# First convolution weights taken in during the attention projection, and a reordered last result

## The chip, the cores and the metric

The kernel runs on one core of a Trainium2 chip. What counts is the time of one execution on the device, in microseconds (us), and less is better. PE is TensorE, the matrix engine; DVE is VectorE, ACT is ScalarE, POOL is GpSimd; SP is the engine that here only issues loads and stores.

## What is computed

Two layers act on 1024 tokens of width 1024, in fp32. The first is windowed attention with a gate, whose output is multiplied by a 2048 x 1024 matrix and added to x. The second is a convolution branch; the part around the change is the end of the first layer and the beginning of the second:

```python
x = x + gate * ((o * silu(z)) @ attn_w_out)        # layer 0: attention
h = rmsnorm(x, norm_g) * (1 + scale) + shift       # layer 1
a, gl, z = split(h @ conv_w_in + conv_b_in, 3)     # 1024 -> 3 x 2048
u = a * sigmoid(gl)
u = conv_depthwise(u, 31 taps) + dw_b
u = silu(layernorm(u)) * silu(z)
x = x + gate * (u @ conv_w_out)
out = rmsnorm(x, final_g)
```

## The kernel before, in words

**Matrix products in three parts.** An fp32 operand is split into a high part (rounded to the matrix engine's fp32r format, a copy on ACT) and a low part (what the rounding left, a subtraction on DVE or POOL). Each product is three matmuls: high x high, high x low, low x high. A 128-wide block of weights is thus loaded ("wraw" for the convolution's input matrix, "wo" for the attention's output matrix), then split into "whi" and "wlo" ("woh" and "wol"). One matmul has 512 columns.

**The attention's output projection (`proj_attn`).** It computes the two halves of the token rows by a scheme of seven products; these are 28 steps: steps i = 0 to 7 are round r = 0, steps 8 to 27 are rounds r = 1 to 5 of four steps (kk = 0 to 3). Each step multiplies one "oz" block (attention output: loaded as "ozf", for some rounds added or subtracted on DVE, split into "ozh" by ACT and "ozl" by DVE) by one "wo" block, into four banks, one for each group of 128 token rows, with six matmuls a bank. `ahead(nl, ns)` loads up to step nl and splits up to step ns. Within `split` the DVE subtraction that makes ozl is not issued at once but put into the list `put_by`; `flush()` issues what is in it. `bgA(r, kk)` is called once for each step and issues background work.

**A finished round.** `first_sum` adds a bank to what earlier rounds left ("part"), `evac0` multiplies by the gate, adds the residual ("xr"), squares and sums on ACT ("junk"; the row sums land in "ssx") and stores the row. `norm0` makes 1/sqrt of the mean square (small operations ms, sq, rr, rq, r on DVE and ACT) and scales the row's two halves into "xn", one half on DVE and one on ACT.

**The last result.** The last product's steps 25 to 27 are held back and run bank by bank (b = 0 to 3), so that a bank's rows can be finished while PE works on the next. After b = 0 and after b = 1 a transposed tile of the first 512 tokens still has to be made.

**Transposed tiles (`turn_in`).** For each of eight k-tiles and each half of the tokens, PE transposes four 128 x 128 pieces of xn into a bank "pso". ACT makes "h2h" (modulated, rounded) and from that "hf", DVE makes "h2l" from the bank and hf. A third pair of transposes has to wait until the first of the two banks is read out. `later` is the list of these to be called.

**The convolution's input projection (`b_mm`).** 48 weight blocks, each for two halves of the tokens, 24 matmuls a block and half. The first five (FIRST) run their first halves, then their second halves; `TURNS` says between which k-steps of blocks 2, 3 and 4 the transposes of the second 512 tokens stand. A block goes to "psg" banks. A gl block is read out by a sigmoid on ACT ("sig"); the a block after it by DVE into "ubuf", whose neighbours POOL then adds ("ubuf" from "ubuf"). The depthwise convolution follows in parts: DVE adds some taps in PSUM ("pss" from "ubuf" with wsum or dww), ACT multiplies the others ("prod"), POOL adds these up ("odd").

**What sets the order.** The order within each engine is fixed when the kernel is built. In the projection (`pin("PVAG")`) PE, DVE, ACT and POOL keep the order of the code; in the first two blocks of the convolution POOL is free to be reordered, and from block 2 on only PE keeps the order. SP's loads may be reordered throughout. Splits of convolution weights have high priority and stand behind the scaling of rows on ACT that came last in the code (`anchor_n`). Tiles come from 45 pages of 1024 words and 6 halves of 528, in the order in which they come free; a load has to wait until its page's last reader is done.

## Time and profile before

| | |
|---|---|
| median of 3 runs | 1689.21 us (1688.74 to 1691.45) |
| the profiled execution | 1689.08 us |
| its span in the trace | 1687.3 us, so 1.8 us lie outside |
| mean granted PE clock | 0.992 |
| busy in the span | PE 1650.8, DVE 1138.4, POOL 931.5, ACT 899.7 us |
| the attention's output projection from step 8 on | about 834 to 953 us |
| convolution blocks 0 and 1, first half | 953.4 to 964.4 us |

Times in the trace run from the start of the span. A row of a timeline gives start, duration, engine, operation, the tile written and the tiles read, and in brackets how long the engine was idle before and which engine's work ended that. A matmul of 512 columns has a row of 0.39 us, but the next one starts about 0.23 us later, since they are pipelined; so PE's pace is read from the distance between starts.

### The profile page before, as it was taken

What the parts mean: (1) busy time and instruction counts of PE and PEld (TensorE: products, weight loads), DVE (VectorE), ACT (ScalarE), POOL (GpSimd) and SP (SyncE); (2) the same over time, 40 slices, a digit from 0 to 9 for tenths busy, and PEclk for the clock granted to TensorE, in tenths of its full rate; (3) what the DMA queues carried; (4) which work ended last, traced back from release to release, by engine and by line L of the source; (5) the groups of instructions that cost most, each with busy time, mean ns of one, the idle gap of its engine ahead of it and who ended that gap; (6) DMA issues with size and microseconds to landing.
All of it is one profiled execution on the core that took longest, in us unless ns stands there. A gap on an engine that the chain in (4) does not pass through costs nothing.

```text
span 1687.3 us, 23985 instructions
## 1 busy us (share of the span) xinstructions
PE 1650.8 (98%) x8244; PEld 1379.1 (82%) x8244; DVE 1138.4 (67%) x2089; ACT 899.7 (53%) x1573; POOL 931.5 (55%) x877
## 2 busy tenths in 40 slices
PE   9999999999999999999999879999999999999998
PEld 6888888888888888888788658888888888888886
DVE  5755544555354554556477789999999998868722
ACT  6644543555355544556228486555656554566831
POOL 0338774686458674772110089999889887130400
PEclk9999999999999999999999989999999999999999
DMA  9435553564356653577778412020211202377971
GB/s 383 167 92 165 157 171 94 166 194 143 96 166 194 197 156 117 170 226 254 273 268 327 152 50 89 13 75 13 76 50 51 82 34 80 130 269 249 320 285 50
DMA packets 151321, 263.53 MB, mean 156 GB/s; under 512 B 46122, under 2 KB 62818, under 8 KB 151200
## 3 DMA queue, kind: packets, MB, share of 16 engines
q1 hardware_dynamic: 142816, 247.84, 43.9%
q10 hardware_dynamic: 8384, 14.16, 2.9%
q8 instruction: 65, 1.06, 0.3%
q14 instruction: 56, 0.46, 0.1%
HBM read 197.19 MB, written 54.27 MB: 149 GB/s over the span
## 4 chain that ended last, share of the span: by engine, by line
PE 85%; DMA 4%; POOL 3%; DVE 3%; ACT 2%; issue 2%; ACTq 0%; SPq 0%; POOLq 0%; DVEq 0%
PE psg L94 45%; PE pso L94 21%; PE pss L94 19%; DMA rope_half<-rope_half 2%; POOL rope_half L94 1%; DVE x_page L94 1%; POOL lhi_half L94 1%; DMA wraw_page<-in_k_win_dram 1%; POOL wlo_page L94 1%; DMA wo_page<-wslow 0%; POOL ql_page L94 0%; DMA araw_page<-in_k_ada_dram 0%; POOL p_page L94 0%; ACT whi_page L94 0%; DVE pss L94 0%
## 5 line engine op out<-in xcount | busy, mean ns | idle before, releaser
L94 POOL TENSOR_TENSOR odd_half<-odd_half,prod_half 128x513 f32<-128x513 f32 (+2 forms) x252 | 317.0, 1264 | 17.7 <-ACT prod_half L94 3.7
L94 PE MATMUL psg<-hh_page,whi_page 128*128 128x512 f32 x600 | 236.8, 395 | 0.0
L94 PE MATMUL psg<-hl_page,whi_page 128*128 128x512 f32 x600 | 234.8, 391 | 0.0
L94 PE MATMUL psg<-hh_page,wlo_page 128*128 128x512 f32 x600 | 234.3, 391 | 0.0
L94 ACT ACTIVATE prod_half<-ubuf,dww 128x513 f32<-128x513 f32 (+2 forms) x252 | 164.9, 674 | 124.8 <-POOL odd_half L94 118.6
L94 POOL TENSOR_TENSOR wlo_page<-wraw_page,whi_page 128x512 fp32r<-128x512 f32 (+1 forms) x104 | 170.8, 1659 | 107.5 <-ACT whi_page L94 103.9
L94 PE MATMUL psg<-h2h_page,whi_page 128*128 128x512 f32 x464 | 183.0, 394 | 11.1 <-ACT whi_page L94 11.1
L94 PE MATMUL psg<-h2h_page,wlo_page 128*128 128x512 f32 x464 | 181.5, 391 | 4.5 <-POOL wlo_page L94 4.5
L94 PE MATMUL psg<-h2l_page,whi_page 128*128 128x512 f32 x464 | 181.3, 391 | 0.0
L94 DVE SCALAR_TENSOR_TENSOR pss<-ubuf,wsum,pss 128x512 f32<-128x512 f32 (+3 forms) x270 | 174.2, 674 | 1.4
L94 DVE SCALAR_TENSOR_TENSOR pss<-ubuf,dww,pss 128x512 f32<-128x512 f32 (+3 forms) x270 | 173.9, 674 | 1.4
L94 ACT ACTIVATE pt<-pss 128x640 fp32r<-128x640 f32 (+1 forms) x128 | 86.5, 676 | 140.3 <-PE pss L94 127.8
L94 POOL TENSOR_SCALAR p_page<-p_page,sc 128x576 f32<-128x576 f32 (+2 forms) x128 | 93.2, 729 | 98.2 <-DVE sc L94 94.0
L94 DVE CUSTOM_DVE_ANT_0 p_page<-pss,mask_page,nsink 128x576 f32<-128x576 f32 (+1 forms) x112 | 90.2, 805 | 75.9 <-PE pss L94 57.3
L94 ACT ACTIVATE p_page<-p_page,sc 128x577 f32<-128x577 f32 (+2 forms) x128 | 96.9, 757 | 68.0 <-DVE sc L94 66.0
L94 PEld LDWEIGHTS psg<-hh_page,wlo_page 128*128 128x128 f32 x600 | 112.7, 188 | 24.4 <-POOL wlo_page L94 0.3
L94 DVE TENSOR_TENSOR pt<-pss,pt 128x640 fp32r<-128x640 f32 (+1 forms) x128 | 100.7, 787 | 44.2 <-ACT pt L94 43.9
L94 PEld LDWEIGHTS psg<-hh_page,whi_page 128*128 128x128 f32 x600 | 112.8, 188 | 19.7 <-ACT hh_page L94 0.3
L94 PEld LDWEIGHTS psg<-hl_page,whi_page 128*128 128x128 f32 x600 | 113.1, 188 | 19.1 <-DVE hl_page L94 0.2
L94 PE MATMUL pso<-h2h_page,whi_page 128*128 128x512 f32 x304 | 118.3, 389 | 0.0
L94 PE MATMUL pso<-h2l_page,whi_page 128*128 128x512 f32 x304 | 118.3, 389 | 0.0
L94 PE MATMUL pso<-h2h_page,wlo_page 128*128 128x512 f32 x304 | 118.3, 389 | 0.0
(294 smaller groups left out, 3980.6 us busy)
## 6 DMA issues: line engine op xcount, KB each, us to landing
wraw_page<-in_k_wconv_dram SPq DMA_DIRECT2D x48, 512.0 KB, 3.3
wraw_page<-in_k_win_dram SPq DMA_DIRECT2D x40, 512.0 KB, 4.2
wo_page<-in_conv_w_out_dram SPq DMA_DIRECT2D x32, 512.0 KB, 5.7
wol_page<-wolC SPq DMA_DIRECT2D x32, 512.0 KB, 5.9
ozf_page<-ozd SPq DMA_DIRECT2D x28, 512.0 KB, 7.1
...
araw_page<-in_k_ada_dram SPq DMA_DIRECT2D x16, 512.0 KB, 10.0
...
```

Of the source, the lines that this page charges most:

```text
L94: r = f(*a, **k)
```

## The change

Four things are changed.

1. The first four blocks of the convolution's weights (0 to 3) are loaded and split at set steps of rounds 1 to 5, by a table of steps. Blocks 4 and 5 are loaded in round 5. Before, blocks 0 and 1 were loaded at the end of round 4 and split in round 5, and blocks 2 to 5 were loaded and split in the loop of the first five blocks, behind the last result. The low parts of blocks 0 to 3 are all made by POOL, in two pieces; before, DVE made those of blocks 0 and 1, and POOL those of 2 to 5. In the blocks' loop there is no split after block 0 any more.
2. `flush()` is called after `ahead` in steps 4 to 7, and after the call of `ahead(10, 9)` ahead of step 8. So step 8's ozl is issued ahead of the first sums of round 0.
3. In the last result, a transposed tile's low part (h2l) comes behind the bank's sums, and the rows are normed by pairs (banks 0 and 1, then 2 and 3) with `rstd_of`, no longer one by one; `rstd_one` is gone.
4. "hf" is one of the 6 halves, no longer a page; the pages of "sig" and "zsb" are taken behind the projection.

```diff
+AHEAD_B = {(1, 3): ("load",), (2, 1): ("split", "load"), (2, 3): ("split", "load"), (3, 1): ("split",), (3, 2): ("load",),
+           (5, 2): ("split", "load", "load")}
...
-    def rstd_one(ssum, n, part):
...
@@ WStream.split
-                    split_lo(self.lo_eng(i), l, r, h)
+                    for a in range(0, KT, KT // 2 if i < 4 else KT):
+                        sl = slice(a, a + (KT // 2 if i < 4 else KT))
+                        split_lo(self.lo_eng(i), *(t[:, sl] for t in (l, r, h)))
@@ proj_attn, round 0
                 ahead(*LOAD_TO[i])
+                flush()
...
         ahead(10, 9)
+        flush()
@@ proj_attn, last result
                             run(block(n, b, acc[b]))
-                        if b < 2:
-                            later.popleft()()
+                        low = later.popleft()(True) if b < 2 else None
                         first_sum(1, 0, b, acc[b], part("m", b), True)
                         evac0(1, 0, b, xr, acc[b])
-                        norm0(1, 0, b)
+                        if low:
+                            low()
+                        if b % 2:
+                            norm0(1, 0, (b - 1, b + 1))
@@ norm0
-        if at is None:
-            r = rstd_of(ss[1], D, 4, ss[0])
-            rows = [(b, r[:, b:b + 1]) for b in range(4)]
-        else:
-            rows = [(at, rstd_one(ss[1][:, at:at + 1], D, ss[0][:, at:at + 1]))]
+        b0, b1 = span
+        r = rstd_of(ss[1][:, b0:b1], D, b1 - b0, ss[0][:, b0:b1])
+        rows = [(b, r[:, b - b0:b - b0 + 1]) for b in range(b0, b1)]
@@ turn_in
-        f = pg.alloc(F32, [1024], "hf")
+        f = hp.alloc(F32, None, "hf")
...
-            stt(H2l[(h, kt)], tv, mod1[:, 8 + kt:9 + kt], fv, ALU.mult, ALU.subtract)
-        pg.free(f)
+
+        def low():
+            with tc.high_priority():
+                stt(H2l[(h, kt)], tv, mod1[:, 8 + kt:9 + kt], fv, ALU.mult, ALU.subtract)
+            hp.free(f)
+
...
+        if hold:
+            return low
+        low()
@@ the convolution's weights
-    wsB = WStream(hp=True, lo_eng=lambda i: V if i < 2 or i % 3 == 0 and i > 3 else G, srcs=...)
+    wsB = WStream(hp=True, lo_eng=lambda i: V if i % 3 == 0 and i > 3 else G, srcs=...)
@@ bgA
-        if (r, kk) == (4, 3):
-            wsB.load()
-            wsB.load()
-        if r == 5:
-            if kk != 1:
-                wsB.split()
+        for what in AHEAD_B.get((r, kk), ()):
+            getattr(wsB, what)()
@@ the first five blocks
         b_mm(i, 0)
         wsB.load()
-        wsB.split()
+        if i:
+            wsB.split()
         wsB.load()
```

PE's own instructions stand in the same order before and after. Three places show how the others move.

**Place 1: DVE at the end of round 0.** The x rows are the first sums of the four banks of step 7; ozl_page_8590 before and ozl_page_8516 after are the low part for step 8 (made from ozf_page_8387 and ozf_page_8385). Before:

```order
L94 TENSOR_TENSOR ozf_page_8387<-ozf_page_8385,ozf_page_8387 128x1024
L94 TENSOR_TENSOR x_page_8542<-psg_7972,part_page_8186 128x512
L94 TENSOR_TENSOR x_page_8542<-psg_7973,part_page_8186 128x512
L94 TENSOR_TENSOR x_page_8557<-pss_8377,part_page_8439 128x512
L94 TENSOR_TENSOR x_page_8557<-pss_8378,part_page_8439 128x512
L94 TENSOR_TENSOR ozf_page_8470<-ozf_page_8468,ozf_page_8470 128x1024
L94 TENSOR_TENSOR ozf_page_8532<-ozf_page_8530,ozf_page_8532 128x1024
L94 TENSOR_TENSOR ozl_page_8590<-ozf_page_8387,ozh_page_8511 128x1024
```

And after:

```order
L96 TENSOR_TENSOR ozf_page_8385<-ozf_page_8383,ozf_page_8385 128x1024
L96 TENSOR_TENSOR ozl_page_8516<-ozf_page_8385,ozh_page_8509 128x1024
L96 TENSOR_TENSOR x_page_8542<-psg_7972,part_page_8186 128x512
L96 TENSOR_TENSOR x_page_8542<-psg_7973,part_page_8186 128x512
L96 TENSOR_TENSOR x_page_8557<-pss_8375,part_page_8437 128x512
L96 TENSOR_TENSOR x_page_8557<-pss_8376,part_page_8437 128x512
L96 TENSOR_TENSOR ozf_page_8468<-ozf_page_8466,ozf_page_8468 128x1024
L96 TENSOR_TENSOR ozl_page_8576<-ozf_page_8468,ozh_page_8569 128x1024
```

Step 8's ozl moved from behind the four sums and two additions to ahead of them; step 9's stands behind its own addition.

**Place 2: DVE in the last result.** psg_7972 is bank 0 and psg_7973 bank 1; h2l are the low parts of the transposed tiles, x and xn the rows. Before, from the first sum of bank 0 to that of bank 1:

```order
L94 SCALAR_TENSOR_TENSOR h2l_page_9440<-pso_9441,mod_611,hf_page_9446 128x512
L94 TENSOR_TENSOR psg_7972<-psg_7972,part_page_8186 128x512
L94 TENSOR_TENSOR psg_7972<-psg_7972,gate_page_8353 128x512
L94 TENSOR_TENSOR x_page_9450<-psg_7972,xr_page_9411 128x512
L94 TENSOR_SCALAR ms_599_9457<-ssx_595_9341,ssx_594_9340 128x1
L94 RECIPROCAL rr_601_9459<-sq_600_9458 128x1
L94 TENSOR_SCALAR rq_602_9460<-rr_601_9459 128x1
L94 TENSOR_SCALAR rq_602_9460<-rq_602_9460,ms_599_9457 128x1
L94 TENSOR_SCALAR r_603_9466<-rq_602_9460,rr_601_9459 128x1
L94 TENSOR_SCALAR xn_page_9468<-x_page_9450,r_603_9466 128x512
L94 SCALAR_TENSOR_TENSOR h2l_page_9440<-pso_9490,mod_611,hf_page_9495 128x512
L94 TENSOR_TENSOR psg_7973<-psg_7973,part_page_8186 128x512
```

After, the same stretch and on to the scaling of both rows:

```order
L96 TENSOR_TENSOR psg_7972<-psg_7972,part_page_8186 128x512
L96 TENSOR_TENSOR psg_7972<-psg_7972,gate_page_8353 128x512
L96 TENSOR_TENSOR x_page_9467<-psg_7972,xr_page_9424 128x512
L96 SCALAR_TENSOR_TENSOR h2l_page_9458<-pso_9459,mod_611,hf_half_9464 128x512
L96 TENSOR_TENSOR psg_7973<-psg_7973,part_page_8186 128x512
L96 TENSOR_TENSOR psg_7973<-psg_7973,gate_page_8353 128x512
L96 TENSOR_TENSOR x_page_9467<-psg_7973,xr_page_9424 128x512
L96 SCALAR_TENSOR_TENSOR h2l_page_9458<-pso_9493,mod_611,hf_half_9498 128x512
L96 SCALAR_TENSOR_TENSOR ms_600_9508<-ssx_595_9358,ssx_594_9357 128x2
L96 RECIPROCAL rr_602_9512<-sq_601_9510 128x2
L96 SCALAR_TENSOR_TENSOR rq_603_9514<-rr_602_9512 128x2
L96 TENSOR_TENSOR rq_603_9514<-rq_603_9514,ms_600_9508 128x2
```

The sums of bank 1 moved ahead of the norm of bank 0, one chain of small operations serves two rows, and each h2l stands behind its bank's sums.

**Place 3: ACT and POOL behind the last scaled row.** sig is the first gl block's sigmoid, the whi rows are weight copies (before: blocks 5, 4, 2, then 3; after: blocks 6, 5, 7, then 4 and 8), h2h_page_9705 before and h2h_page_9693 after the first transposed tile of the second 512 tokens. ACT before:

```order
L94 ACTIVATE sig_page_8375<-psg_9595,vt 128x512
L94 ACTIVATE whi_page_9848<-wraw_page_9693 128x1024
L94 ACTIVATE whi_page_9771<-wraw_page_9687 128x1024
L94 ACTIVATE whi_page_9623<-wraw_page_9621 128x1024
L94 ACTIVATE odd_half_9656<-ubuf,vt,dww 128x249
L94 ACTIVATE prod_half_9658<-ubuf,dww 128x249
L94 ACTIVATE prod_half_9661<-ubuf,dww 128x249
L94 ACTIVATE prod_half_9664<-ubuf,dww 128x249
L94 ACTIVATE prod_half_9667<-ubuf,dww 128x249
L94 ACTIVATE prod_half_9670<-ubuf,dww 128x249
L94 ACTIVATE whi_page_9689<-wraw_page_9627 128x1024
L94 ACTIVATE prod_half_9719<-ubuf,dww 128x249
L94 ACTIVATE prod_half_9722<-ubuf,dww 128x249
L94 ACTIVATE h2h_page_9705<-pso_9707,mod_611 128x512
```

ACT after:

```order
L96 ACTIVATE sig_page_9591<-psg_9593,vt 128x512
L96 ACTIVATE whi_page_9836<-wraw_page_9681 128x1024
L96 ACTIVATE whi_page_9759<-wraw_page_9437 128x1024
L96 ACTIVATE whi_page_9908<-wraw_page_9763 128x1024
L96 ACTIVATE odd_half_9646<-ubuf,vt,dww 128x249
L96 ACTIVATE prod_half_9648<-ubuf,dww 128x249
L96 ACTIVATE prod_half_9651<-ubuf,dww 128x249
L96 ACTIVATE prod_half_9654<-ubuf,dww 128x249
L96 ACTIVATE prod_half_9657<-ubuf,dww 128x249
L96 ACTIVATE prod_half_9660<-ubuf,dww 128x249
L96 ACTIVATE whi_page_9677<-wraw_page_9435 128x1024
L96 ACTIVATE h2h_page_9693<-pso_9695,mod_611 128x512
L96 ACTIVATE whi_page_10132<-wraw_page_9840 128x1024
L96 ACTIVATE h2h_page_9693<-pso_9723,mod_611 128x512
```

POOL at the same place, before:

```order
L94 TENSOR_TENSOR wol_page_8631<-wo_page_8580,woh_page_8629 128x512 x2
L94 TENSOR_TENSOR ubuf<-ubuf 128x263
L94 TENSOR_TENSOR wlo_page_9849<-wraw_page_9693,whi_page_9848 128x1024
L94 TENSOR_TENSOR wlo_page_9772<-wraw_page_9687,whi_page_9771 128x1024
L94 TENSOR_TENSOR wlo_page_9624<-wraw_page_9621,whi_page_9623 128x1024
L94 TENSOR_TENSOR odd_half_9656<-odd_half_9656,prod_half_9658 128x249
L94 TENSOR_TENSOR wlo_page_9690<-wraw_page_9627,whi_page_9689 128x1024
L94 TENSOR_TENSOR odd_half_9656<-odd_half_9656,prod_half_9661 128x249
```

and after:

```order
L96 TENSOR_TENSOR wlo_page_8908<-wraw_page_8823,whi_page_8907 128x512 x2
L96 TENSOR_TENSOR wlo_page_9026<-wraw_page_8912,whi_page_9025 128x512 x2
L96 TENSOR_TENSOR wlo_page_9431<-wraw_page_9066,whi_page_9430 128x512 x2
L96 TENSOR_TENSOR wlo_page_9760<-wraw_page_9437,whi_page_9759 128x1024
L96 TENSOR_TENSOR wlo_page_9909<-wraw_page_9763,whi_page_9908 128x1024
L96 TENSOR_TENSOR ubuf<-ubuf 128x263
L96 TENSOR_TENSOR odd_half_9646<-odd_half_9646,prod_half_9648 128x249
L96 TENSOR_TENSOR wlo_page_9678<-wraw_page_9435,whi_page_9677 128x1024
L96 TENSOR_TENSOR odd_half_9646<-odd_half_9646,prod_half_9651 128x249
```

The copies for blocks 2 and 3 are gone from here, and those for blocks 6, 5 and 7 stand in their place ahead of the first products. On POOL the low parts of blocks 5 and 7 stand ahead of the first ubuf, which before came first.

23 lines of the change are left out of this document (7 added, 16 removed).

## The prediction

> **What bounds the kernel now.** I read the page's busy row first, then PE's waits, then PE's timeline around each of them, and then the timelines of the engines that were waited for. The page's row of busy time, and the waits of PE from 820 to 1010 us (how long in all, how often, the longest):
>
> ```profile
> PE 1650.8 (98%) x8244; PEld 1379.1 (82%) x8244; DVE 1138.4 (67%) x2089; ACT 899.7 (53%) x1573; POOL 931.5 (55%) x877
> PE psg L94 <- ACT whi_page L94: 11.1, 1, 11.1
> PE psg L94 <- POOL wlo_page L94: 4.5, 1, 4.5
> PE pso L94 <- DVE ozl_page L94: 3.7, 1, 3.7
> PE pso L94 <- DVE h2l_page L94: 0.8, 2, 0.4
> ```
>
> PE bounds the kernel. Its matmuls are the same after the change, so a gain can only come from its waits, and from what follows a wait. The timeline of PE shows both:
>
> ```profile
> 834.60 0.39 PE L94 MATMUL pso<-woh_page,ozh_page 128*128 128x512 f32 x1
> 834.82 0.39 PE L94 MATMUL pso<-wol_page,ozh_page 128*128 128x512 f32 x1
> 838.95 0.79 PE L94 MATMUL pso<-woh_page,ozl_page 128*128 128x512 f32 x1 [3.74 <-DVE ozl_page L94]
> 839.54 0.63 PE L94 MATMUL pso<-woh_page,ozh_page 128*128 128x512 f32 x1
> 839.96 0.63 PE L94 MATMUL pso<-wol_page,ozh_page 128*128 128x512 f32 x1
> ...
> 953.48 0.39 PE L94 MATMUL psg<-h2h_page,whi_page 128*128 128x512 f32 x1
> ...
> 964.13 0.39 PE L94 MATMUL psg<-h2h_page,wlo_page 128*128 128x512 f32 x1
> 975.64 0.79 PE L94 MATMUL psg<-h2h_page,whi_page 128*128 128x512 f32 x1 [11.12 <-ACT whi_page L94]
> 976.23 0.63 PE L94 MATMUL psg<-h2l_page,whi_page 128*128 128x512 f32 x1
> 981.32 0.80 PE L94 MATMUL psg<-h2h_page,wlo_page 128*128 128x512 f32 x1 [4.46 <-POOL wlo_page L94]
> 981.91 0.63 PE L94 MATMUL psg<-h2h_page,whi_page 128*128 128x512 f32 x1
> 982.34 0.63 PE L94 MATMUL psg<-h2l_page,whi_page 128*128 128x512 f32 x1
> ...
> 985.71 0.39 PE L94 MATMUL psg<-h2l_page,whi_page 128*128 128x512 f32 x1
> ```
>
> A matmul normally starts 0.23 us after the last one (834.60 to 834.82). The row at 953.48 is the first matmul of the convolution's block 0, so bank 3 of the last result is finished there. From 834.82 to 838.95 it is 4.1 us, so 3.9 too long; then about eight are 0.2 us too slow (839.54 to 839.96: 0.42), 1.7 us together. I call this stall A: 5.6 us. From 964.13 to 975.64 it is 11.5 us (11.3 too long), from 976.23 to 981.32 5.1 us (4.9 too long), and up to 985.7 matmuls stand 0.43 us apart (981.91 to 982.34): 2.6 us too long in all. With the two h2l waits of 0.8 us this is stall B: 11.3 + 4.9 + 2.6 + 0.8 = 19.6 us. If all went and nothing came in its place, the gain would be 25.2 us.
>
> The third view is the busy time by stretches (us, then PE, PEld, DVE, ACT, POOL, and PE's granted clock):
>
> ```profile
> 964.00:1004.00 40.00, 23.61 (x105) 17.98 (x104) 32.12 (x68) 30.14 (x53) 26.14 (x25) 0.79 0.12 41
> 1004.00:1400.00 396.00, 396.00 (x1748) 327.89 (x1747) 387.85 (x589) 233.62 (x328) 355.01 (x259) 1.00 0.16 56
> ```
>
> Behind stall B, PE does not wait for 396 us, but DVE is busy for 387.85 of them (98%) and POOL for 355. In the convolution there is a second engine that is nearly the bound. This is what limits the gain from B.
>
> **Stall A: `flush()`.** DVE, ACT and POOL around it:
>
> ```profile
> 835.40 2.35 DVE L94 TENSOR_TENSOR ozf_page<-ozf_page,ozf_page 128x1024 f32<-128x1024 f32 x2
> 837.67 4.58 DVE L94 TENSOR_TENSOR ozl_page<-ozf_page,ozh_page 128x1024 fp32r<-128x1024 f32 x3
> ...
> 837.66 1.04 ACT L94 ACTIVATE woh_page<-wo_page 128x1024 fp32r<-128x1024 f32 x1
> ...
> 828.21 2.53 POOL L94 TENSOR_TENSOR wol_page<-wo_page,woh_page 128x512 fp32r<-128x512 f32 x2 [19.11 <-ACT woh_page L94]
> 838.78 12.57 POOL L94 TENSOR_TENSOR wol_page<-wo_page,woh_page 128x512 fp32r<-128x512 f32 x6 [8.04 <-ACT woh_page L94]
> ```
>
> PE waits for step 8's ozl (837.67, behind the sums and two additions), which now stands ahead of the sums. So PE goes through step 8 without a wait: 24 matmuls from 834.6, to 840.0. Step 9 is late next: its addition still stands behind the last sum (835.4), ACT's woh runs from 837.7 to 838.7, and POOL's two halves of wol start at 838.8. Alone such a half takes 1.27 us (828.21), beside a busy DVE 2.1 us (838.78: 12.57 by 6), so they are done at 840.9 and 843.0 at most, while PE wants them at 840.3 and 841.6. The new wait is 0 to 2.1 us; I take 2.0, the value beside a busy DVE, since DVE stays busy there. It is under the 3.7 us behind which matmuls were slow. Gain from A: 5.6 - 2.0 = 3.6 us.
>
> **Stall B: weights split earlier, and the last result reordered.** DVE's first and last operations in the last result, and what follows on ACT and POOL:
>
> ```profile
> 946.82 1.22 DVE L94 TENSOR_TENSOR wlo_page<-wraw_page,whi_page 128x1024 fp32r<-128x1024 f32 x1 [0.78 <-ACT whi_page L94]
> 948.24 0.75 DVE L94 SCALAR_TENSOR_TENSOR h2l_page<-pso,mod,hf_page 128x512 fp32r<-128x512 f32 x1 [0.20 <-ACT hf_page L94]
> 948.90 0.69 DVE L94 TENSOR_TENSOR psg<-psg,part_page 128x512 f32<-128x512 f32 x1
> 960.89 0.69 DVE L94 TENSOR_TENSOR pss<-pss,part_page 128x512 f32<-128x512 f32 x1
> 965.66 0.69 DVE L94 TENSOR_TENSOR pss<-pss,part_page 128x512 f32<-128x512 f32 x1
> 972.78 0.75 DVE L94 SCALAR_TENSOR_TENSOR ubuf<-psg,vt,sig_page 128x512 f32<-128x512 f32 x1 [2.27 <-ACT sig_page L94]
> 974.36 0.54 DVE L94 TENSOR_SCALAR pss<-ubuf,wsum,dwb 128x248 f32<-128x248 f32 x1 [0.31 <-POOL ubuf L94]
> ...
> 970.77 1.28 ACT L94 ACT_TABLE_LOAD   x1
> 972.65 2.94 ACT L94 ACTIVATE whi_page<-wraw_page 128x1024 fp32r<-128x1024 f32 x3
> 975.98 2.06 ACT L94 ACTIVATE prod_half<-ubuf,dww 128x249 f32<-128x249 f32 x5
> ...
> 973.68 0.65 POOL L94 TENSOR_TENSOR ubuf<-ubuf 128x263 f32<-128x263 f32 x1 [122.33 <-DVE ubuf L94]
> 974.28 6.98 POOL L94 TENSOR_TENSOR wlo_page<-wraw_page,whi_page 128x1024 fp32r<-128x1024 f32 x3
> ```
>
> Before, a row costs 4.8 us (sum to sum, 960.89 to 965.66), the last xn is out at 970.77, when ACT loads its table, and block 2's whi comes third behind that on ACT, its wlo third on POOL. After, blocks 2 and 3 are split in the projection or early in the last result; POOL's 122 us of idle time and ACT's gaps there hide this (eight halves of 1.27 to 2.1 us, four copies of about 1 us). Were that cover gone, they would cost 10 to 21 us, on an engine that PE waits for only through wol. DVE's two weight subtractions of 1.2 us go.
>
> I walk the last result with these durations. The first sum stood at 948.9 behind the two subtractions, a wait of 0.8 us for the second one's copy, and an h2l of 0.7 us; without them it starts at 948.9 - 2.4 - 0.8 - 0.7 = 945.0. Three operations a bank take 2.2 us, an h2l 0.7, and a norm, from a bank's third operation to the last xn, 3 us (967.8 to 970.8), with a second row 3.5. That gives 950.1 for bank 1's sums, 953.6 for the first pair, 958.0 for bank 3's sums (PE ended bank 3 at 953.5) and, a norm later, about 961.2 for the last xn, 9.6 us earlier than before. The table load and the sigmoid take 1.9 us (970.77 to 972.65) and end at 963.1, before PE is done with block 1 (964.4). The waits of 11.1 and 4.5 us and the slow matmuls go.
>
> What is late next? ACT has whi of blocks 6, 5 and 7 ahead of the first products: to 966.1. POOL has wlo of blocks 5 and 7 (2.3 us each, 6.98 by 3) ahead of the first ubuf: 965.1 to 969.7, ubuf until 970.3. So DVE's second tap starts at 970.3, where it was 974.36: only 4.1 us earlier. On ACT an odd, the five products, block 4's copy, h2h, block 8's copy, the second h2h, a sigmoid and hf follow. I give those without a row of their own the sigmoid's 0.6 to 0.7 us: 966.1 + 0.5 + 2.1 + 1.0 + 0.7 + 1.0 + 0.7 + 0.7 + 0.7 = 973.5, and the first h2l on DVE is done at 974.2. PE reaches the third transposes, which need that bank, at about 970.7 (24 matmuls and two sets of transposes behind 964.4). This is a new wait of up to 3.5 us (nothing if ACT gets through sooner). The fourth transposes wait for an hf that now waits for POOL's odd sums in the halves: about 1.0 us, an estimate from POOL's order, and the second half of block 0 about 0.7 us, one h2l. Together 5.2 us, with bounds 0 and 8.
>
> A clock loss of 1.7 us followed the 3.74 us gap of stall A, while the waits for h2l of 0.4 us show none. 3.5 us is nearer the former; but my 3.5 us is itself an upper value, so I take half, 0.9 us. The Trainium skill ("TensorE: Matmul & The Clock Gate", Part 1) says that PE falls to half its clock after an idle window of about 3.4 us that runs freely, and needs about as long to come back. The 3.74 us gap agrees with that. By this rule the new wait would drop the clock or not, as the window falls; with a drop the time below would be 1675.4 in place of 1674.6 us.
>
> Gain from B: 19.6 - 5.2 - 0.9 = 13.5 us. With A, PE has 17.1 us at about 1005.
>
> **What the convolution gives back.** DVE begins its taps only 4.1 + 3.6 = 7.7 us earlier, and has 8.15 us of idle time in the 396 us to catch up with. At the end of the convolution stands
>
> ```profile
> 1436.12 1.23 DVE L94 TENSOR_TENSOR wlo_page<-wraw_page,whi_page 128x1024 fp32r<-128x1024 f32 x1
> 1443.47 6.67 DVE L94 TENSOR_TENSOR v_page<-v_page,pso 128x512 f32<-128x512 f32 x11 [6.13 <-PE pso L94]
> ```
>
> DVE waits 6.1 us for PE there. So if DVE catches up by nothing, 7.7 + 6.1 = 13.8 us are kept; if it catches up, all 17.1. I take 14.6, near the lower end, since a DVE at 98% has little to catch up with. 1689.08 - 14.6 = 1674.5 for the profiled execution; the median of the runs is 0.1 above it, so 1674.6 us.
>
> **The rivals.** Bounds for a verdict: 0.2% is 3.4 us, about what a measurement of this kernel can tell from no change.
>
> First: *DVE and POOL bound the convolution from the start.* If the banks run out in the middle, the 6.1 us at the end cannot be used, and the gain is what DVE's start gains: 7.7 us, 1681.4 (6 to 11 us: 1678 to 1683). For it: 98% busy, and POOL's wlo ahead of ubuf. Against: 396 us without one wait of PE, so that there is some room.
>
> Second: *the new waits do not come*, because ACT and POOL get through sooner or the reordered taps let DVE catch up: 19 to 24 us, 1665 to 1670. Against: the products' and weight copies' places in the order of ACT.
>
> Third: *the stall only moves.* If the transposes and their low parts, and not the weights, are what PE needs, block 2's wait of 11 us turns up at the third transposes. It would have to be over 16 us for no change; my walk gives 3.5. The time would be about 1689 us.
>
> Fourth, slower: *block 6's weights come late.* ACT's copy of them stands first behind the sigmoid, ahead of everything that PE waits for, and its load stands in SP's queue behind one that waits until PE has finished bank 3 (953.5), and waits itself for the first xn (953.5). Landing takes
>
> ```profile
> wraw_page<-in_k_wconv_dram SPq DMA_DIRECT2D x48, 512.0 KB, 3.3
> ```
>
> 3.3 us, so it is there at 957, or at 963 if three such loads share the queue; ACT wants it at 963.1. Every us later is one more at the third transposes. From 14.6 us later on (978) it is slower than before; 20 us later would give 1689.1 + 5.4 = 1694.5. Against it: that is six times the row's 3.3 us.
>
> **How the numbers follow.** Forecast (12 to 18 us, 1671 to 1677): 0.50. First rival: 0.25. Second: 0.12. Third, within 0.2%: 0.07. Fourth and the like: 0.06. Range: 1667.5 (the greater part of the second rival) to 1684 (all of the first); outside are the third and fourth rivals and the second's end, under 0.2. Faster by over 0.2%: 0.50 + 0.25 + 0.12 = 0.87; same 0.07; slower 0.06.
>
> **What would show it.** In the profile after: no PE wait for whi or wlo at block 2; at step 9 a wait for wol of about 2 us in place of 3.7 for ozl; the last xn about 10 us earlier; a wait for h2l of 1 to 3.5 us at the third transposes; DVE's idle time ahead of the vsum matmuls shorter than 6.1 us. It is wrong if PE waits in the convolution behind 1005 us for ubuf, or for whi of block 6 or later.

## The result, and the profile after

| | before | after |
|---|---|---|
| median, us | 1690.07 (4 runs, 1688.74 to 1691.45) | 1675.65 (4 runs, 1674.76 to 1676.35) |
| profiled execution, us | 1689.08 | 1676.35 |
| span in the trace, us | 1687.3 | 1674.6 |
| mean granted PE clock | 0.992 | 0.996 |

The ratio is 0.9914, with a 95% interval of 0.9897 to 0.9932. By the medians that is a gain of 14.4 us; the spans of the two profiled executions differ by 12.7 us, and the account below goes by these. Executions of one kernel lie up to 2.7 us apart in this table, so a difference of 1 us between two single traces says little. The prediction was 1674.6 us. It was near, but its terms were wrong in opposite directions, as the trace shows.

The page's row of busy time, and the waits of PE from 815 to 1010 us (how long in all, how often, the longest), in the changed kernel:

```profile
PE 1650.0 (99%) x8244; PEld 1379.0 (82%) x8244; DVE 1130.9 (68%) x2077; ACT 900.9 (54%) x1571; POOL 932.1 (56%) x883
PE pso L96 <- DVE h2l_page L96: 4.8, 2, 2.5
PE pso L96 <- POOL wol_page L96: 1.2, 1, 1.2
PE psg L96 <- DVE ozl_page L96: 1.1, 1, 1.1
PE psg L96 <- ACT woh_page L96: 1.0, 1, 1.0
```

The waits for whi (11.1 us) and wlo (4.5) are gone, and that for ozl at step 8 (3.7). The wol wait of step 9 is there, as foreseen. But three waits stand in the middle of the projection, where the kernel before had none. PE's timeline gives their places:

```profile
842.97 0.50 PE L96 MATMUL pso<-wol_page,ozh_page 128*128 128x512 f32 x1 [1.25 <-POOL wol_page L96]
...
887.00 0.50 PE L96 MATMUL psg<-woh_page,ozh_page 128*128 128x512 f32 x1 [0.97 <-ACT woh_page L96]
894.32 0.50 PE L96 MATMUL psg<-woh_page,ozl_page 128*128 128x512 f32 x1 [1.11 <-DVE ozl_page L96]
...
927.63 0.66 PE L96 MATMUL pso<-ident,xn_page 128*128 128x128 f32 x4 [2.52 <-DVE h2l_page L96]
928.94 0.63 PE L96 MATMUL pss<-woh_page,ozh_page 128*128 128x512 f32 x1
929.37 0.63 PE L96 MATMUL pss<-wo_page,ozh_page 128*128 128x512 f32 x1
...
956.69 0.39 PE L96 MATMUL psg<-h2h_page,whi_page 128*128 128x512 f32 x1
...
976.37 1.07 PE L96 MATMUL pso<-ident,xn_page 128*128 128x128 f32 x4 [2.24 <-DVE h2l_page L96]
977.67 0.63 PE L96 MATMUL psg<-h2l_page,whi_page 128*128 128x512 f32 x1
978.09 0.63 PE L96 MATMUL psg<-h2h_page,wlo_page 128*128 128x512 f32 x1
```

The number to take from this is the start of block 0, 956.69. Before it was 953.48. So PE comes out of the projection 3.2 us later than before, not 3.6 us earlier: the waits of 0.97, 1.11 and 2.52 us and the matmuls at half pace behind the last of them (928.94 to 929.37) have used up what step 8 gave, and more. Of these 3.2 us, 0.6 were there at step 8 already: PE reached it at 835.18, before at 834.60. That is no effect of the change that the runs show, since in the runs below PE reaches step 8 at 834.5 to 836.2, with and without the flushes. From step 8 to block 0 it took 121.5 us, 2.6 more than the 118.9 before. From block 0 on, however, PE gains 15.9 us, since it ends 12.7 us earlier. The one wait left there is the foreseen one, at the third transposes (2.24 us, and slow matmuls again).

Why do these transposes wait? ACT, POOL and DVE of the changed kernel behind the last result, each in order of time:

```profile
962.88 1.28 ACT L96 ACT_TABLE_LOAD   x1
964.17 0.69 ACT L96 ACTIVATE sig_page<-psg,vt 128x512 f32<-128x512 f32 x1
964.75 2.94 ACT L96 ACTIVATE whi_page<-wraw_page 128x1024 fp32r<-128x1024 f32 x3
...
974.82 0.72 ACT L96 ACTIVATE hf_half<-h2h_page,bcol 128x512 f32<-128x512 f32 x1
...
966.83 4.86 POOL L96 TENSOR_TENSOR wlo_page<-wraw_page,whi_page 128x1024 fp32r<-128x1024 f32 x2 [16.17 <-ACT whi_page L96]
...
972.33 0.54 DVE L96 TENSOR_SCALAR pss<-ubuf,wsum,dwb 128x248 f32<-128x248 f32 x1 [3.30 <-POOL ubuf L96]
975.57 0.75 DVE L96 SCALAR_TENSOR_TENSOR h2l_page<-pso,mod,hf_half 128x512 fp32r<-128x512 f32 x1 [0.63 <-ACT hf_half L96]
```

The three weight copies start as soon as the sigmoid is done, so their loads had landed: block 6's weights are not late. POOL's two low parts (4.86 us) stand ahead of the first sum of ubuf's neighbours, and DVE waits 3.30 us for that. The hf for the transposes is done only at 975.5, behind copies and products on ACT, and the h2l behind that. This is the chain that the prediction walked.

The stretches of the changed kernel (PE, PEld, DVE, ACT, POOL, clock), and the end of the convolution, where DVE writes vsum, PE multiplies it and DVE goes on with the product (first the kernel before, L94, then the changed one, L96):

```profile
964.00:1004.00 40.00, 37.76 (x175) 30.93 (x174) 31.50 (x66) 33.63 (x59) 30.55 (x32) 0.96 0.10 32
1004.00:1400.00 396.00, 396.00 (x1748) 327.89 (x1747) 384.20 (x589) 232.81 (x324) 348.17 (x255) 1.00 0.16 56
...
1435.39 0.69 DVE L94 TENSOR_TENSOR vsum_page<-vsum_page,v_page 128x512 f32<-128x512 f32 x1
1442.41 1.02 PE L94 MATMUL pso<-vsum_page,ones 128*128 128x512 f32 x2
...
1428.21 0.69 DVE L96 TENSOR_TENSOR vsum_page<-vsum_page,v_page 128x512 f32<-128x512 f32 x1
1429.71 1.02 PE L96 MATMUL pso<-vsum_page,ones 128*128 128x512 f32 x2
1430.77 3.67 DVE L96 TENSOR_TENSOR v_page<-v_page,pso 128x512 f32<-128x512 f32 x6 [1.86 <-PE pso L96]
```

Of the first 40 us PE was busy for 23.61 before and is for 37.76 now. In the 396 us behind them PE has no wait in either kernel, and nothing of the lead is given back. DVE's idle time behind vsum fell from 6.13 to 1.86 us. More exactly, vsum was ready 6.3 us before PE took it (1436.08 to 1442.41) and is ready 0.8 us before now (1428.90 to 1429.71).

### The profile page after: what moved, and what is told of

It is laid out like the page before. It is cut to its first block, busy times and chain, and to the rows that moved or that the text cites. A ratio compares the mean times of both kernels' runs of the same rounds, so it can differ in the third digit from the quotient of the medians.

```text
span 1674.6 us, 23971 instructions
## 1 busy us (share of the span) xinstructions
PE 1650.0 (99%) x8244; PEld 1379.0 (82%) x8244; DVE 1130.9 (68%) x2077; ACT 900.9 (54%) x1571; POOL 932.1 (56%) x883
## 4 chain that ended last, share of the span: by engine, by line
PE 85%; DMA 4%; DVE 3%; POOL 3%; issue 2%; ACT 2%; ACTq 0%; SPq 0%; POOLq 0%; DVEq 0%
PE psg L96 46%; PE pso L96 21%; PE pss L96 19%; DMA rope_half<-rope_half 2%; DMA wo_page<-wsums 1%; POOL rope_half L96 1%; DVE ozl_page L96 1%; POOL lhi_half L96 1%; DVE ozf_page L96 1%; DVE x_page L96 1%; DMA dww_raw<-in_ada_w_dram 0%; DMA ozf_page<-ozd 0%; ACT ozh_page L96 0%; POOL ql_page L96 0%; DMA xr_page<-in_x_dram 0%
## 5 line engine op out<-in xcount | busy, mean ns | idle before, releaser
L96 POOL TENSOR_TENSOR odd_half<-odd_half,prod_half 128x513 f32<-128x513 f32 (+2 forms) x252 | 312.5, 1248 | 31.6 <-ACT prod_half L96 18.7
L96 POOL TENSOR_TENSOR wlo_page<-wraw_page,whi_page 128x512 fp32r<-128x512 f32 (+1 forms) x110 | 179.1, 1645 | 214.9 <-ACT whi_page L96 165.0
L96 PE MATMUL psg<-hh_page,whi_page 128*128 128x512 f32 x600 | 236.8, 395 | 0.0
L96 PE MATMUL psg<-hl_page,whi_page 128*128 128x512 f32 x600 | 234.8, 391 | 0.0
L96 PE MATMUL psg<-hh_page,wlo_page 128*128 128x512 f32 x600 | 234.3, 391 | 0.0
L96 ACT ACTIVATE prod_half<-ubuf,dww 128x513 f32<-128x513 f32 (+2 forms) x252 | 165.3, 674 | 105.1 <-POOL odd_half L96 101.6
L96 PE MATMUL psg<-h2h_page,whi_page 128*128 128x512 f32 x464 | 182.5, 393 | 0.0
L96 PE MATMUL psg<-h2h_page,wlo_page 128*128 128x512 f32 x464 | 181.1, 390 | 0.0
L96 PE MATMUL psg<-h2l_page,whi_page 128*128 128x512 f32 x464 | 181.1, 390 | 0.0
L96 DVE SCALAR_TENSOR_TENSOR pss<-ubuf,wsum,pss 128x512 f32<-128x512 f32 (+3 forms) x270 | 173.5, 673 | 1.0
L96 DVE SCALAR_TENSOR_TENSOR pss<-ubuf,dww,pss 128x512 f32<-128x512 f32 (+3 forms) x270 | 173.4, 673 | 1.0
L96 ACT ACTIVATE pt<-pss 128x640 fp32r<-128x640 f32 (+1 forms) x128 | 86.5, 676 | 139.1 <-PE pss L96 126.4
L96 POOL TENSOR_SCALAR p_page<-p_page,sc 128x576 f32<-128x576 f32 (+2 forms) x128 | 93.4, 730 | 97.5 <-DVE sc L96 96.4
L96 DVE CUSTOM_DVE_ANT_0 p_page<-pss,mask_page,nsink 128x576 f32<-128x576 f32 (+1 forms) x112 | 90.2, 805 | 75.6 <-PE pss L96 57.1
L96 ACT ACTIVATE p_page<-p_page,sc 128x577 f32<-128x577 f32 (+2 forms) x128 | 96.9, 757 | 68.3 <-DVE sc L96 66.4
L96 PEld LDWEIGHTS psg<-hh_page,wlo_page 128*128 128x128 f32 x600 | 112.7, 188 | 24.5 <-POOL wlo_page L96 0.3
L96 DVE TENSOR_TENSOR pt<-pss,pt 128x640 fp32r<-128x640 f32 (+1 forms) x128 | 100.7, 787 | 43.9 <-ACT pt L96 43.5
L96 PEld LDWEIGHTS psg<-hh_page,whi_page 128*128 128x128 f32 x600 | 112.8, 188 | 19.7 <-ACT hh_page L96 0.3
L96 PEld LDWEIGHTS psg<-hl_page,whi_page 128*128 128x128 f32 x600 | 113.1, 188 | 19.0 <-DVE hl_page L96 0.2
L96 PE MATMUL pso<-h2h_page,whi_page 128*128 128x512 f32 x304 | 118.3, 389 | 0.0
L96 PE MATMUL pso<-h2l_page,whi_page 128*128 128x512 f32 x304 | 118.3, 389 | 0.0
L96 PE MATMUL pso<-h2h_page,wlo_page 128*128 128x512 f32 x304 | 118.3, 389 | 0.0
```

Of the source, the lines that this page charges most:

```text
L96: r = f(*a, **k)
```

## The experiments

Theory A: taking the weights in early is not free in the projection; GpSimd's subtractions beside VectorE, ACT's copies, or the pages held cost PE 6 to 7 us by block 0. Its rival is that the flushes or the new order of the last result make the new waits. Theory B: the lead behind block 0 is limited only by the order on ACT and POOL at the first transposes. Its rival is the prediction's first one, that DVE bounds the convolution, so that a larger lead would be lost there.

All runs, each with the kernel before on the same chip. "Block 0" is the start of its first matmul in the trace, "from step 8" the time from step 8's first matmul to it. The second is the better measure of the projection, since PE's arrival at step 8 differs by up to 1.7 us between these single executions.

| kernel | block 0, us | from step 8, us | span, us | median, us | before there, us | ratio (95% interval) |
|---|---|---|---|---|---|---|
| before | 953.48 | 118.9 | 1687.3 | | 1690.07 | |
| after | 956.69 | 121.5 | 1674.6 | 1675.65 | 1690.07 | 0.9914 (0.9897 to 0.9932) |
| e1 flushes alone | 950.30 | 115.0 | 1684.1 | 1686.27 | 1690.65 | 0.9974 (0.9964 to 0.9984) |
| e2 weights alone | 959.95 | 125.2 | 1687.3 | 1689.00 | 1690.65 | 0.9989 (0.9980 to 0.9998) |
| e3 order alone | 954.75 | 120.2 | 1679.4 | 1681.56 | 1690.65 | 0.9943 (0.9929 to 0.9956) |
| e4 after without flushes | 961.72 | 125.5 | 1679.1 | 1679.80 | 1690.65 | 0.9937 (0.9924 to 0.9951) |
| e5 after without weights | 950.99 | 115.0 | 1675.9 | 1677.36 | 1689.62 | 0.9925 (0.9912 to 0.9939) |
| e6 weights late | 950.58 | 115.0 | 1672.9 | 1674.93 | 1689.62 | 0.9912 (0.9899 to 0.9926) |
| e7 copies behind first turns | 956.59 | 121.3 | 1678.8 | 1679.88 | 1689.62 | 0.9941 (0.9928 to 0.9953) |
| e8 e6 and e7 together | 949.76 | 115.0 | 1672.9 | 1675.49 | 1689.62 | 0.9917 (0.9904 to 0.9931) |
| e9 copies behind all turns | 950.39 | 115.0 | 1667.7 | 1669.61 | 1691.39 | 0.9876 (0.9861 to 0.9890) |
| e10 e9 with hf in pages | 950.03 | 115.1 | 1666.3 | 1668.61 | 1691.39 | 0.9870 (0.9855 to 0.9885) |
| e11 e6 with early loads | 950.90 | 115.0 | 1673.3 | 1674.62 | 1691.39 | 0.9903 (0.9887 to 0.9920) |
| e12 after without low parts | 952.63 | 117.4 | 1670.5 | 1672.38 | 1690.63 | 0.9893 (0.9877 to 0.9910) |

### The change in its parts: e1 to e5

**e1**, the kernel before with the flushes.

```diff
@@ before, proj_attn
                 ahead(*LOAD_TO[i])
+                flush()
...
         ahead(10, 9)
+        flush()
```

> The kernel before with the two calls of flush alone. Theory: the matrix engine's new waits of the projection in the changed kernel (about 1.0 us for woh, 1.1 for ozl, 2.5 for h2l with slow matmuls behind it) come from the weights that are loaded and split there. Then this kernel has the whole gain of stall A, 3.5 us by the traces, and keeps it to the end: about 1686.5 us. Rival: they come because the matrix engine runs 3.5 us ahead of engines that had no slack. Then the same waits stand here, the gain is lost by 930 us, and the time is that of before within 1 us: about 1689.

The waits of PE:

```profile
PE psg L94 <- ACT whi_page L94: 11.1, 1, 11.1
...
PE pso L94 <- POOL wol_page L94: 1.2, 1, 1.2
```

PE starts block 0 3.2 us earlier and keeps just that to the end (spans 1687.3 and 1684.1). From step 8 on it gains 3.9 us. None of the new waits in the projection is there, so the flushes do not make them.

**e2**, the kernel before with the early weights alone (the table of steps, the low parts on POOL in pieces, sig and zsb taken late).

```diff
@@ before, bgA
-        if (r, kk) == (4, 3):
-            wsB.load()
-            wsB.load()
-        if r == 5:
-            if kk != 1:
-                wsB.split()
+        for what in AHEAD_B.get((r, kk), ()):
+            getattr(wsB, what)()
@@ the first five blocks
-        wsB.split()
+        if i:
+            wsB.split()
```

> The kernel before with the weights of blocks 0 to 3 loaded and split in the projection (and the two pages taken later), without flush and with the last result in its old order. Theory: weights alone do not do it, since block 2 needs the bank that the first sigmoid reads, and that stands behind the last scaled row (972.8 us in the trace of before). The matrix engine then waits about 8 us there for the sigmoid in place of 11.1 and 4.5 for weights: 4 to 8 us gained, about 1683. Rival: the weights are what was waited for, and the gain of B comes from them alone: 12 us or more, under 1678.

The ratio's interval reaches 0.9998, so nearly nothing came of it. Block 0 starts 6.5 us later than before, and the wait at block 2 is now one for the sigmoid, which stands behind the last norm:

```profile
977.99 0.79 PE L96 MATMUL psg<-h2h_page,whi_page 128*128 128x512 f32 x1 [7.00 <-ACT sig_page L96]
```

The expectation was too good: it had seen the later sigmoid, but not the price in the projection.

**e3**, the kernel before with the order alone.

```diff
@@ before, last result
-                        if b < 2:
-                            later.popleft()()
+                        low = later.popleft()(True) if b < 2 else None
                         first_sum(1, 0, b, acc[b], part("m", b), True)
                         evac0(1, 0, b, xr, acc[b])
-                        norm0(1, 0, b)
+                        if low:
+                            low()
+                        if b % 2:
+                            norm0(1, 0, (b - 1, b + 1))
@@ turn_in
-        f = pg.alloc(F32, [1024], "hf")
+        f = hp.alloc(F32, None, "hf")
```

> The kernel before with the last result reordered and normed by pairs (and hf in the halves) alone. Theory: the last scaled row comes 9 us earlier, so block 2's high part comes about 9 us earlier, and its low part, third on GpSimd, about 7 us earlier: the two waits shrink from 15.6 to about 7 us and 7 to 10 us are gained, about 1681. Rival: the weights alone set block 2, and the order saves nothing that the matrix engine sees: 1689.

7.9 us of span, as expected: the wait for whi falls from 11.1 to 2.6 us, while that for wlo is still 4.1. Block 0 comes 1.3 us later than before, but not because of the order: behind the same wait of 3.7 us at step 8, 13 matmuls stood 0.42 to 0.43 us apart here and 6 in the kernel before.

**e4**, the changed kernel without the flushes.

```diff
@@ after, proj_attn
                 ahead(*LOAD_TO[i])
-                flush()
...
         ahead(10, 9)
-        flush()
```

> The changed kernel without the two calls of flush. Theory (the projection's new waits come from the weights): the wait of 3.7 us for ozl of step 8 is back with its slow matmuls, 5.6 us, and the 1.3 us for wol goes; later waits stay for the most part: 2 to 4 us slower than the changed kernel, about 1679. Rival (they come from running ahead): what flush wins is lost by 930 us anyway, and the time is that of the changed kernel within 1 us, 1675.7.

4.5 us of span are lost again (1.1 of them before step 8), where 2 to 4 were expected; the ozl wait of 3.7 is back, and ozl 1.1, woh 0.7 and h2l stay. Against e3, which differs from it in the weights only, block 0 comes 5.3 us later from step 8 on.

**e5**, the changed kernel with the weights taken in as before.

```diff
@@ after, bgA
-        for what in AHEAD_B.get((r, kk), ()):
-            getattr(wsB, what)()
+        if (r, kk) == (4, 3):
+            wsB.load()
+            wsB.load()
+        if r == 5:
+            if kk != 1:
+                wsB.split()
```

> The changed kernel without the early weights: flush and the reordered last result alone, the weights of blocks 0 to 5 loaded and split as before. If the parts simply add up, it gains 4.4 + 9.1 us by the runs of each alone: about 1677 us. Theory: the early weights bring little in the end, since what they save at block 2 (2.6 us for the high part and 4.1 for the low part are left in the run with the order alone, with slow matmuls behind) they take in the projection (about 6.5 us): within 2 us of the changed kernel, 1675 to 1678. Rival: the early weights are the core of the gain: 1681 or more.

```profile
PE psg L94 <- POOL wlo_page L94: 4.2, 1, 4.2
PE psg L94 <- ACT whi_page L94: 2.6, 1, 2.6
```

The waits in the projection are gone, those for whi and wlo are back with 6.8 us. The median is 1.7 us above that of the changed kernel. So the early weights are worth only 1.3 us of span (0.5 from step 8 on), and the intervals of the two ratios overlap; flushes and order bring 11.4 of the 12.7 us. Three pairs that differ in the early weights alone (e2 and before, after and e5, e4 and e3) put their price from step 8 to block 0 at 6.3, 6.5 and 5.3 us. The pairs differ in how many slow matmuls followed their waits. e1 and e5, with and without the order, take the same 115.0 us, so the order costs nothing there.

### What in the early weights costs: e6, e11, e12

**e6**, the changed kernel with the first blocks loaded and split late, in rounds 4 and 5.

```diff
-AHEAD_B = {(1, 3): ("load",), (2, 1): ("split", "load"), (2, 3): ("split", "load"), (3, 1): ("split",), (3, 2): ("load",),
-           (5, 2): ("split", "load", "load")}
+AHEAD_B = {(4, 3): ("load", "load"), (5, 0): ("split", "load"), (5, 2): ("split", "split", "load", "load")}
@@ the first five blocks
-        if i:
-            wsB.split()
+        wsB.split()
```

> The changed kernel with the weights taken in later: blocks 0 and 1 loaded at the end of round 4 as before, blocks 0 to 2 split at steps (5, 0) and (5, 2), block 3 in the loop of the first five blocks. Theory: the projection's new waits (woh 1.0, ozl 1.1, h2l 2.5, slow matmuls 1.5 us, about 6 us) go with the weights of rounds 1 to 3, and block 2 does not wait: 1669 to 1672 us. Block 3's low part, now behind others on GpSimd, may take 1 to 3 us of it. Rival: the convolution on VectorE bounds what comes behind, and gives it back: 1675.

```profile
PE pso L95 <- DVE h2l_page L95: 5.9, 2, 5.3
PE pso L95 <- POOL wol_page L95: 1.2, 1, 1.2
```

Block 0 starts at 950.58, 6.1 us earlier than in the changed kernel, and only step 9's wait for wol is left in the projection. But the time is 1674.93, not 1669 to 1672. That is the rival's number, yet not by its mechanism, since PE does not wait behind 1005 us: PE reaches the third transposes sooner, and the wait there grows from 2.24 to 5.34 us. The expectation had taken that wait as fixed. POOL shows why it is not:

```profile
965.51 0.67 POOL L95 TENSOR_TENSOR ubuf<-ubuf 128x263 f32<-128x263 f32 x1
966.12 5.85 POOL L95 TENSOR_TENSOR wlo_page<-wraw_page,whi_page 128x1024 fp32r<-128x1024 f32 x3
971.93 0.71 POOL L95 TENSOR_TENSOR odd_half<-odd_half,prod_half 128x249 f32<-128x249 f32 x1
```

Now three weight blocks (5.85 us) stand between the first ubuf and the first sum of products. On ACT, the hf of the third transposes starts behind that sum.

**e11**, e6 with the loads of blocks 0 and 1 early, but their splits late.

```diff
-AHEAD_B = {(4, 3): ("load", "load"), (5, 0): ("split", "load"), (5, 2): ("split", "split", "load", "load")}
+AHEAD_B = {(1, 3): ("load",), (2, 1): ("load",), (5, 0): ("split", "load"), (5, 2): ("split", "split", "load", "load")}
```

> The kernel with the late weights, with the loads of blocks 0 and 1 alone put back to where the change has them (rounds 1 and 2), their splits still in round 5. Tells apart what makes the matrix engine wait in the projection. If the loads do it (SyncE's queue and the pages they hold): waits for woh, ozl or h2l of 1 us or more stand in rounds 3 to 5 again, 1677 to 1680 us. If the splits do it (ScalarE's copies, GpSimd's low parts beside VectorE): no such wait, and the time of the kernel with the late weights, 1675.

Block 0 starts at 950.90 and the projection has no wait but step 9's: early loads of blocks 0 and 1 cost nothing. That leaves the splits, with the pages that split blocks hold; the early loads of blocks 2 and 3 were not tried alone.

**e12**, the changed kernel in which POOL only writes zeros for the low parts of blocks 0 to 2 (their subtraction is left out).

```diff
@@ after, WStream.split
-                        split_lo(self.lo_eng(i), *(t[:, sl] for t in (l, r, h)))
+                        if i < 3:
+                            G.memset(l[:, sl].bitcast(F32), 0.0)
+                        else:
+                            split_lo(self.lo_eng(i), *(t[:, sl] for t in (l, r, h)))
```

> The changed kernel, in which GpSimd writes zeros in place of the low parts of the convolution's weight blocks 0 to 2 (so it leaves those low parts out; PE's matmuls, ACT's copies, the loads and the pages are as they were). Theory: GpSimd's subtractions beside VectorE slow VectorE's ozl, its products and its additions (1.2 us became 2.3, 0.7 became 1.7), and this makes the waits for ozl (1.1 us) and woh (1.0). Then both go or fall under 0.3 us each, and the products of DVE in 885 to 895 take 0.7 us again. The h2l wait of 2.5 us at 927 hangs on a late load of ozf, whose page frees when an ozl is done; if it too comes from slow VectorE work, it falls under 1 us, and PE begins block 0 at 951 to 952 instead of 956.7: 1669 to 1671 us. If only the first two go, 953.5 to 954.5 and 1672.5 to 1674 us. Rival: ACT's copies and the scarce pages alone make the waits. Then all three waits stay as they are, PE begins block 0 at 956 to 957, and the time is 1675 to 1676.5 us.

In the changed kernel, DVE and POOL around the first two new waits:

```profile
876.63 2.28 DVE L96 TENSOR_TENSOR ozl_page<-ozf_page,ozh_page 128x1024 fp32r<-128x1024 f32 x1 [1.21 <-ACT ozh_page L96]
...
888.32 1.78 DVE L96 TENSOR_TENSOR x_page<-x_page,gate_page 128x512 f32<-128x512 f32 x1
890.13 1.67 DVE L96 TENSOR_TENSOR x_page<-x_page,xr_page 128x512 f32<-128x512 f32 x1
...
874.94 2.89 POOL L96 TENSOR_TENSOR wlo_page<-wraw_page,whi_page 128x512 fp32r<-128x512 f32 x2 [22.64 <-PE pso L96]
888.03 3.21 POOL L96 TENSOR_TENSOR wlo_page<-wraw_page,whi_page 128x512 fp32r<-128x512 f32 x2 [10.21 <-issue]
```

The same two stretches in e12:

```profile
876.67 1.23 DVE L96 TENSOR_TENSOR ozl_page<-ozf_page,ozh_page 128x1024 fp32r<-128x1024 f32 x1 [1.21 <-ACT ozh_page L96]
...
887.30 0.68 DVE L96 TENSOR_TENSOR x_page<-x_page,gate_page 128x512 f32<-128x512 f32 x1
888.02 0.69 DVE L96 TENSOR_TENSOR x_page<-x_page,xr_page 128x512 f32<-128x512 f32 x1
...
875.00 1.00 POOL L96 MEMSET wlo_page<- 128x512 f32 x2 [15.23 <-issue]
885.94 0.99 POOL L96 MEMSET wlo_page<- 128x512 f32 x2 [9.94 <-PE pss L96]
```

And its waits:

```profile
PE pso L96 <- DVE h2l_page L96: 3.8, 2, 2.2
PE pso L96 <- POOL wol_page L96: 1.2, 1, 1.2
PE psg L96 <- DVE part_page L96: 0.4, 2, 0.3
```

Beside POOL's subtraction ozl took 2.28 us instead of 1.23, and each of the two row operations 1.1 and 1.0 us longer. The 1.05 us pass on: the next ozh on ACT starts at 884.95 instead of 883.93, woh behind it, and PE waits 0.97 us for woh. The other 2.1 stand ahead of the ozl that PE waits 1.11 us for. With the subtractions gone, so are these 3.1 us and both waits; the third new wait, for h2l, shrinks from 2.52 to 1.52 us, and no slow matmuls follow it. Block 0 starts 4.1 us earlier (952.63) and the span is 4.1 us shorter. This fell between the two outcomes that the theory had named, and it rules out that copies alone make the waits. One thing speaks for caution: a memset does not read the raw block, so its page comes free sooner, and POOL is busy for less time. For the waits for woh and ozl the durations on DVE account by themselves; for the h2l wait they do not.

So 4.1 of the 6.5 us go with POOL's subtractions. The other 2.4 (117.4 us from step 8 against 115.0 in e6) are for the most part what is left of the h2l wait (1.52) and a wait for part (0.4). In the changed kernel ACT's h2h, from which this h2l comes, stands behind an ozh that waits for a load:

```profile
923.01 1.06 ACT L96 ACTIVATE ozh_page<-ozf_page 128x1024 fp32r<-128x1024 f32 x1 [2.32 <-DMA ozf_page<-ozd]
```

In e12 this wait is still 1.92 us. What makes the load late, ACT's copies or the pages that split blocks hold, is not told apart. POOL's one remaining subtraction, of block 3 at 944.60, comes too late for it. In e6 POOL subtracts for blocks 0 to 2 between 938 and 950 us, and PE waits for nothing there. Two row operations of DVE take 1.67 and 1.78 us beside it again (938.74 and 940.33), but PE does not need them at once; and the sums of the last result, which read one operand from a bank, take 0.69 to 0.70 us from 944.44 to 949.77, beside the subtractions as elsewhere.

### Where the lead goes: e7 to e10

**e7**, the changed kernel with ACT's copies of the blocks from 5 on ordered behind the hf of the first two transposed tiles; **e8** is the same on top of e6.

```diff
@@ WStream.split
-                    after(act(h, r, AF.Copy), anchor_n)
+                    after(act(h, r, AF.Copy), anchor_h if i > 4 else anchor_n)
@@ turn_in
-            act(fv, H2h[(h, kt)].bitcast(F32), AF.Identity, bias=bcol[:, kt:kt + 1])
+            hf_at = act(fv, H2h[(h, kt)].bitcast(F32), AF.Identity, bias=bcol[:, kt:kt + 1])
+            if h and kt < 2:
+                anchor_h[:] = [hf_at]
```

> The changed kernel with ScalarE's copies of the weights of block 5 and later put behind the hf of the first transposed tiles of the second half of the tokens, no longer ahead of the first products. Theory: the wait of 2.2 us at the third transposes and the slow matmuls behind it (1.5 us) come from these copies and from the low parts on GpSimd ahead of ubuf: 3 to 4 us faster than the changed kernel, 1672. Rival: VectorE's convolution is the bound, and the time is that of the changed kernel, 1675.7, with the wait moved elsewhere.

> The two edits of the last two runs together. Theory: they add up, 9 to 10 us faster than the changed kernel, 1665 to 1668 us. Rival: VectorE's convolution bounds from 1005 us on and gives the second part back: 1670 to 1672.

Both missed. In e7 the wait at the third transposes fell only to 1.59 us and one of 4.10 came at a later pair; it is 4.2 us slower than the changed kernel. In e8 PE waits four times for h2l, 6.2 us in all. The copies, and DVE's low part of block 6 with them, were only pushed between the next transposes, where they stand in the way again.

**e9**, e6 with these copies behind every transposed tile, and the splits of the blocks from 5 on in the loop of the second halves; **e10** is e9 with hf in pages again, as before the change.

```diff
@@ turn_in
-            act(fv, H2h[(h, kt)].bitcast(F32), AF.Identity, bias=bcol[:, kt:kt + 1])
+            anchor_h[:] = [act(fv, H2h[(h, kt)].bitcast(F32), AF.Identity, bias=bcol[:, kt:kt + 1])]
@@ the first five blocks, first halves
-        wsB.split()
+        if i < 2:
+            wsB.split()
@@ the first five blocks, second halves
         wsB.done(i)
+        if i < 3:
+            wsB.split()
```

> The kernel with the late weights and ScalarE's copies put back (the run before), with the copies of block 5 and later now behind the last of the eight transposed tiles' hf, no longer behind the second, and split in the loop of the second halves. Theory: the waits of 2.5 and 2.0 us for h2l at the fifth and sixth transposes in the run before come from three copies in a row on ScalarE and from VectorE's low part of block 6 (3.2 us beside GpSimd); they go, and 3 to 5 us are gained: 1670 to 1672 us. Rival: the chain of hf, GpSimd's odd sums and the six halves is what the transposes wait for: no gain, 1675.

> The same kernel with hf in a page again, as before the change. Theory: an hf in a half waits until GpSimd has added up the product that had it; in a page it does not, so what is left of the waits for h2l at the third and later transposes goes: 1 to 3 us faster than the run with halves, 1668 to 1670 us. Rival: the halves cost nothing by now: the same time.

In e9 the waits of 2.45 and 1.98 us are gone, two of 0.9 are left, and the time is a little better than expected. In e10 one wait of 1.3 us for h2l is left. Its stretch behind 1004 us, and its end of the convolution; the last row is that of e9:

```profile
1004.00:1400.00 396.00, 396.00 (x1749) 328.01 (x1748) 386.88 (x582) 235.20 (x326) 353.51 (x257) 1.00 0.16 54
...
1420.50 0.69 DVE L95 TENSOR_TENSOR vsum_page<-vsum_page,v_page 128x512 f32<-128x512 f32 x1
1421.47 1.02 PE L95 MATMUL pso<-vsum_page,ones 128*128 128x512 f32 x2
...
1422.80 1.10 PE L95 MATMUL pso<-vsum_page,ones 128*128 128x512 f32 x2 [0.24 <-DVE vsum_page L95]
```

The span is 21.0 us shorter than before and 8.3 us shorter than after the change. PE still has no wait in the 396 us of the convolution, with DVE busy for 386.88 of them. So the rival of theory B fell for these leads: the convolution takes one of 21 us without giving any back. But nothing is left over. In e10 vsum is ready 0.3 us before PE takes it (1421.19 to 1421.47), and in e9 PE already waits 0.24 us for it. Whether a larger lead would be kept is not shown. e9 and e10 differ by 1.0 us and their intervals overlap; whether hf in halves costs anything stays open. Both are faster than the changed kernel: they were timed on another chip than it, but the ratios' intervals do not touch (e9's ends at 0.9890, the changed kernel's begins at 0.9897).

## Why the number was right, and the steps that were not

**Stall A: right.** Step 8's wait went, step 9's wol wait came with 1.25 us where 2.0 were taken, and e1 measures the flushes at 3.9 us from step 8 to block 0 (3.2 us of span), where 3.6 were predicted.

**Weights in the projection: wrong, 6.5 us where nothing was priced.** The step that failed reads "POOL's 122 us of idle time and ACT's gaps there hide this". It priced the moved work on the engines that do it and asked whether they are idle. They are; but beside POOL's subtraction DVE's operations took longer (2.28 for 1.23 us), and DVE makes the ozl and the sums that PE waits for. This is 4.1 of the 6.5 us (e12); the cause of the other 2.4 stays open. From step 8 to block 0 PE took 2.6 us more than before, where 3.6 less were predicted. The warning stood in a row that the prediction itself used: wol at 1.27 us a half alone and 2.1 beside a busy DVE. It was read as a price for POOL only. The Trainium skill ("SBUF — State Buffer", Who interferes with whom) says that a DVE instruction with two SBUF inputs contends with a GpSimd instruction that reads SBUF, and not with one that only writes it. The runs agree: beside the subtraction 2.28, 1.78 and 1.67 us, and with memsets in its place 1.23, 0.68 and 0.69. In e6 the sums with one operand in a bank took 0.69 to 0.70 beside it. This rule spoke against this part of the change and was not weighed.

**Stall B: right in its mechanism, 2.4 us too small.** The waits for whi and wlo went, and the new wait came at the third transposes by the predicted chain. In size: the transposes 2.24 us (3.5 predicted), slow matmuls 1.6 (0.9), and the fourth transposes and the second half of block 0 nothing (1.7). That leaves 15.9 us, where 13.5 were predicted. By e4 the slow matmuls could as well not have come: there a wait of the same 2.24 us was followed by none. The last xn was out at 962.88, 7.9 us earlier than before (9.6 predicted), because PE itself came late (in e6, where it came 6.1 us sooner, at 960.16).

**Given back: wrong, 2.5 us predicted, none measured.** The prediction let DVE, busy for 98% of the time, catch up by hardly anything: 13.8 us kept without any catching up, and 14.6 taken. DVE's second tap began at 972.33, only 2.0 us earlier than before. From there to the end of vsum DVE took 5.2 us less (456.6 for 461.7), and 5.5 us came from the time by which vsum is ready ahead of PE (6.3 before, 0.8 now). These three make the 12.7 us. Where in the 457 us DVE caught up by 5.2 was not traced. A lead of 21 us (e10) is kept too, and with it the end of the convolution has no such time left.

**The sum.** 14.6 predicted, less 6.2 for the projection (3.6 us to be gained, 2.6 lost), less 0.6 for the later arrival at step 8, plus 2.4 and 2.5 for the other two: 12.7 us, the measured difference of the spans. The time was near by luck: one large error was met by two of the other sign, and the median lies 0.7 us below the profiled execution.

**Of the rivals**, the first (DVE and POOL bound the convolution) is refuted by e9 and e10 for leads up to 21 us, while e9's wait for vsum shows that it is near there. The second's premise, no new wait, did not hold for the change but does nearly for e10, whose 1668.61 lies in its 1665 to 1670. The third came only as the 2.24 us that the forecast had itself, and the fourth not at all.
